# The opening of a conformer block's first FFN: x by token tile, the first adaLN pair on TensorE, paired first weight tiles, and a longer ramp of row tiles

## The chip, the cores and the metric

The kernel runs on one core of one Trainium2 chip. Its time is device microseconds per execution, the median of several runs. Beside the times stands one profiled execution, whose trace gives every instruction's start, duration and what it waited for. The engines are named as in the profile: PE (TensorE matmul), PEld (TensorE weight load), DVE (VectorE), ACT (ScalarE), POOL (GpSimd) and SP, whose queue issues all the loads here.

## What is computed

One conformer block on 256 tokens of width 2048, in float32. A conditioning vector `c` gives nine modulation vectors (adaLN): shift, scale and gate for each of the three parts.

```python
c_act = silu(c)                                     # [1, 2048]
ada = c_act @ w_ada + b_ada                         # nine vectors of 2048
h = modulate(rms_norm(x, ffn1_norm), sh1, sc1)      # h * (1 + sc1) + sh1
x = x + 0.5 * g1 * swiglu(h, w_gu, w_down)          # FFN 1: 2048 -> 2 x 5632 -> 2048
h = modulate(rms_norm(x, mix_norm), shm, scm)
x = x + gm * hybrid_mixer(h, ...)                   # differential attention and causal convolution
h = modulate(rms_norm(x, ffn2_norm), sh2, sc2)
x = x + 0.5 * g2 * swiglu(h, ...)                   # FFN 2
```

The first product of FFN 1 needs the normalised x (a sum over all 2048 channels of a token), transposed to channels on partitions, and for its first 128 channels 128 values of the scale `sc1` and 128 of the shift `sh1`. Each of these values is a sum over all 2048 entries of `silu(c)`.

## The kernel before

**Products.** A float32 product with weights is three passes of a rounded type: each operand is split into a high part and its exact remainder, and hi\*hi, hi\*lo and lo\*hi are accumulated (`mm3`, lines 232 to 234). A weight tile is four row tiles of 128 x 512, 1 MB, loaded into one of four buffers `raw` (line 217); per two row tiles ACT casts the high part (line 222) and DVE subtracts it to get the low part (line 224). With two token tiles a row tile costs PE 2 x 3 products.

**adaLN tiles.** An adaLN tile is 128 outputs by 2048 inputs, 1 MB; there are 144, in the order in which they are needed: for each 128-channel tile a scale and a shift. `ada(j)` loads a tile into a `raw` buffer (line 151), multiplies it on DVE with `silu(c)`, which lies on every partition (`c_bc`), and sums along the row (line 152). Every second tile DVE adds the biases (line 156); `modulation` makes the scale column from it (line 184). `ada_until(j)` issues all tiles up to j, `ada_share(r, limit)` adds r to a credit and issues a tile for each whole one.

**The opening.** `c` is loaded as one row, spread to all partitions by products with a row of ones (line 110) and passed through silu on ACT (line 112). Then x is loaded by column quarters for both token tiles (line 569), with sums of squares on ACT and DVE (lines 252, 255), then the constants, among them the biases and the identity for transposes. `Norm.begin` makes the reciprocal root (lines 268, 128, 129), scales x (line 280) and transposes it on PE (line 285); `Norm.tile` modulates one 128-channel tile of one token tile on DVE (line 293), casts it on ACT (line 295) and takes the remainder on DVE (line 296).

**FFN.** The first projection is cut into 22 chunks of 512 columns (256 gate, 256 up), each with a 2048-row weight matrix, that is four pieces of four row tiles. Stage A takes the first row tiles of every chunk and evacuates the sum into `parts` (line 345): 1, 1, 1, 2, 2, 2, 3 (five times), then 4 row tiles (`EXT`), since the modulations of the first piece's four row tiles arrive one after the other. Loads go three chunks ahead of the products (`AHEAD`). Then `n_a2` = 8 chunks, from the fourth on, get the rest of their first piece and their second piece (the last `n_a3` = 2 of them the third too) and DVE adds this to `parts` (line 412); then all chunks are finished. `pieces()` makes the activations of the second and third piece (lines 282, 285, 314, 317 to 319) as soon as their adaLN tiles are issued.

**Order.** The tile framework's planner orders each engine's instructions, by program order and by its own estimate of when operands are ready; each engine then works in that order. `tc.issue_after(ins)` puts instructions of a block behind `ins` on its engine. A tile name's buffers are reused in turn, and a load into one waits until its last reader is done. `blk` buffers (32 of 4 KB per partition) hold x, parts, activations and more.

Of the kernel before, what the change touches and what calls it, by code (L numbers as in the profile page):

```python
# [16 lines left out]
F32 = mybir.dt.float32  # L17
# [30 lines left out]
# columns of the packed small parameters  # L48
# [17 lines left out]
def block_kernel(ctx: ExitStack, tc: tile.TileContext, x_in, c_in, pos_in, w_ada, small, w_gu1, w_dn1,  # L66
# [3 lines left out]
    blkp = ctx.enter_context(tc.tile_pool(name="blkp", bufs=32))  # L70
# [30 lines left out]
    # ---------------------------------------------------------------- constants  # L101
    c_bc = const.tile([P, D], F32, name="c_bc")
    c_row = [blk([1, 1024]) for _ in range(2)]
    ones_r = tmp([1, P])
    nc.gpsimd.memset(ones_r, 1.0)
    for i in range(2):
        nc.sync.dma_start(out=c_row[i], in_=c_in[:, i * 1024:(i + 1) * 1024])
        for j in range(2):
            pc = acc_tile()
            nc.tensor.matmul(pc, ones_r, c_row[i][:, j * 512:(j + 1) * 512], start=True, stop=True)  # L110
            o = (2 * i + j) * 512
            nc.scalar.activation(out=c_bc[:, o:o + 512], in_=pc, func=AF.Silu)
    cst = const.tile([P, NCOLS], F32, name="cst")
    pos_i = const.tile([P, NT], I32, name="pos_i")

# [8 lines left out]
    nc.gpsimd.memset(half, -0.5)  # L124

    def rstd_of(ss, n, count, eps):
# [16 lines left out]
    # ---------------------------------------------------------------- adaLN projections  # L143
    ada_cols = {}

    def ada(j):
        g = j // 8
        if j % 8 == 0:
            ada_cols[g] = const.tile([P, 8], F32, name=f"ada{g}")
        raw = rawp.tile([P, D], F32, tag="raw", name=nm("raw"))  # L150
        nc.sync.dma_start(out=raw, in_=w_ada[j])
# [6 lines left out]
    ada_next = [0]  # L158
# [18 lines left out]
    def modulation(base, k, norm):  # L177
        """Scale and shift columns of the 128-channel tile k."""
# [9 lines left out]

    def gate(base, scale):
        """The gate's 2048 values on every partition, as four [P, 512] views (through DRAM)."""  # L190
# [755 lines left out]
```

## Time and profile before

| | |
|---|---|
| time, median of 3 runs | 1874.07 us (1871.6 to 1874.78) |
| profiled execution: span from the first to the last instruction | 1872.4 us |
| what the runs' median has beside that span | 1.7 us |
| mean granted TensorE clock | 0.995 |
| first product of FFN 1 | at 21.79 us |
| moved by DMA | 495.92 MB, 265 GB/s |

The profiled execution's own time is not listed beside its span; the three runs' times are what there is, and the span lies within them. In the rows, L224 is line 224 of the kernel, `wlo<-raw,whi` are the written and the read buffers by name, and `[2.41 <-ACT whi L222]` is idle time of the engine before the instruction and what ended it. In rows of stretches the busy times stand by engine, then the granted clock as a share of full speed, the DMA engines' share and GB/s.

### The profile page before, as it was taken

The numbers are of one execution on the slowest core, as the hardware profiler recorded it, in microseconds if no ns is written. First come the engines' busy times: TensorE is split into PE (matmuls) and PEld (weight loads), VectorE is DVE, ScalarE is ACT, GpSimd is POOL, SyncE is SP. The second block draws the span as 40 slices with busy tenths as digits, with TensorE's granted clock in tenths as the row PEclk, the third lists the DMA queues.
The fourth block names the chain that finished last, engine by engine and source line by source line (L and its number), as shares of the span: only waits on it lengthen the run. The fifth ranks groups of instructions, "written<-read, shape, count | busy, mean of one in ns | idle before, by whom it ended". The sixth has DMA issues, their size and how long they took to land.

```text
span 1872.4 us, 21954 instructions
## 1 busy us (share of the span) xinstructions
PE 1838.1 (98%) x8295; PEld 1510.8 (81%) x8295; DVE 1439.3 (77%) x1921; ACT 905.5 (48%) x1363; POOL 30.9 (2%) x34
## 2 busy tenths in 40 slices
PE   6999999999999999999999999999999999999999
PEld 3788888888888888778877788888888888888887
DVE  6779889988888777789999688775877755544443
ACT  4654354444444434454876555654444444433332
POOL 0000000000000000000110100000000000000000
PEclk9999999999999999999999899999999999999999
DMA  8888978888898888646343696895777755555552
GB/s 312 341 315 328 364 272 327 330 326 329 317 345 330 335 340 333 226 170 210 137 158 138 241 344 257 328 355 202 274 285 272 275 197 180 190 215 205 201 212 79
DMA packets 72141, 495.92 MB, mean 265 GB/s; under 512 B 8114, under 2 KB 8290, under 8 KB 14052
## 3 DMA queue, kind: packets, MB, share of 16 engines
q1 hardware_dynamic: 72036, 494.53, 71.5%
q8 instruction: 65, 1.06, 0.2%
q14 instruction: 40, 0.33, 0.1%
HBM read 492.37 MB, written 2.12 MB: 264 GB/s over the span
## 4 chain that ended last, share of the span: by engine, by line
PE 91%; DVE 5%; ACT 2%; issue 1%; DMA 1%; POOL 1%; POOLq 0%; ACTq 0%; DVEq 0%
PE acc L233 29%; PE acc L234 29%; PE acc L232 29%; DVE wlo L224 1%; DVE blk L596 1%; PE tp L426 1%; DMA raw<-in_w_ada_dram 1%; PE acc L677 1%; DVE raw L152 1%; PE tp L285 0%; ACT whi L222 0%; PE acc L110 0%; PE tp L740 0%; POOL rs L129 0%; ACT tmp L632 0%
## 5 line engine op out<-in xcount | busy, mean ns | idle before, releaser
L222 ACT CAST whi<-raw 128x1024 fp32r<-128x1024 f32 (+1 forms) x624 | 645.7, 1042 | 773.1 <-PE acc L234 665.9
L224 DVE TENSOR_TENSOR wlo<-raw,whi 128x1024 fp32r<-128x1024 f32 (+1 forms) x624 | 747.5, 1210 | 349.6 <-ACT whi L222 348.6
L232 PE MATMUL acc<-whi,blk 128*128 128x512 f32 x2464 | 966.2, 394 | 12.2 <-ACT whi L222 6.2
L233 PE MATMUL acc<-wlo,blk 128*128 128x512 f32 x2464 | 965.1, 392 | 3.5 <-DVE wlo L224 3.5
L234 PE MATMUL acc<-whi,blk 128*128 128x512 f32 x2464 | 964.8, 392 | 0.5 <-DVE blk L319 0.5
L232 PEld LDWEIGHTS acc<-whi,blk 128*128 128x128 f32 x2464 | 464.2, 189 | 110.0 <-ACT whi L222 8.3
L233 PEld LDWEIGHTS acc<-wlo,blk 128*128 128x128 f32 x2464 | 464.9, 189 | 101.6 <-DVE wlo L224 6.7
L234 PEld LDWEIGHTS acc<-whi,blk 128*128 128x128 f32 x2464 | 464.8, 189 | 97.3 <-DVE blk L319 0.9
L152 DVE CUSTOM_DVE_ANT_0 raw<-raw,c_bc 128x2048 f32<-128x2048 f32 x144 | 328.9, 2285 | 5.2 <-DMA raw<-in_w_ada_dram 5.2
L596 DVE SCALAR_TENSOR_TENSOR blk<-blk,cst,blk 128x256 f32<-128x256 f32 x240 | 100.9, 483 | 0.0
L345 ACT COPY blk<-acc 128x512 f32<-128x512 f32 x88 | 51.0, 589 | 84.6 <-PE acc L234 81.3
L422 DVE TENSOR_TENSOR blk<-acc,blk 128x512 f32<-128x512 f32 x88 | 56.8, 684 | 0.5 <-PE acc L234 0.5
L233 PE MATMUL acc<-blk,blk 128*128 128x512 f32 x96 | 37.4, 391 | 0.5 <-DVE blk L224 0.5
L232 PE MATMUL acc<-blk,blk 128*128 128x512 f32 x96 | 37.8, 394 | 0.0
L234 PE MATMUL acc<-blk,blk 128*128 128x512 f32 x96 | 37.4, 390 | 0.0
L424 DVE TENSOR_TENSOR blk<-blk 128x256 f32<-128x256 f32 x88 | 34.7, 420 | 0.8 <-ACT blk L423 0.7
L423 ACT ACTIVATE blk<-blk 128x256 f32<-128x256 f32 x88 | 33.3, 409 | 2.6 <-DVE blk L422 1.7
L244 DVE TENSOR_TENSOR blk<-tp,blk 128x512 fp32r<-128x512 f32 x44 | 30.0, 685 | 0.9 <-ACT blk L243 0.8
L224 DVE TENSOR_TENSOR blk<-raw,blk 128x1024 fp32r<-128x1024 f32 x24 | 28.7, 1221 | 0.8 <-ACT blk L222 0.8
L426 PEld LDWEIGHTS tp<-cst,blk 128*128 128x128 f32 x176 | 21.6, 140 | 5.6 <-DVE blk L244 0.3
L243 ACT CAST blk<-tp 128x512 fp32r<-128x512 f32 x44 | 25.3, 581 | 1.6 <-PE tp L426 1.6
L426 PE MATMUL tp<-cst,blk 128*128 128x128 f32 x176 | 26.0, 272 | 0.0
(134 smaller groups left out, 624.1 us busy)
## 6 DMA issues: line engine op xcount, KB each, us to landing
raw<-in_w_gu_dram SPq DMA_DIRECT2D x165, 1024.0 KB, 4.9
raw<-in_w_ada_dram SPq DMA_DIRECT2D x144, 1024.0 KB, 5.7
raw<-in_w_dn_dram SPq DMA_DIRECT2D x88, 1024.0 KB, 4.8
raw<-in_w_in_dram SPq DMA_DIRECT2D x40, 1024.0 KB, 4.8
raw<-in_w_out_dram SPq DMA_DIRECT2D x16, 1024.0 KB, 5.4
raw<-in_w_gu_dram SPq DMA_DIRECT2D x8, 768.0 KB, 7.0
raw<-in_w_gu_dram SPq DMA_DIRECT2D x6, 512.0 KB, 6.6
blk<-gate_line SPq DMA_DIRECT2D x6, 512.0 KB, 6.6
```

The lines of the kernel that those rows point to most:

```text
L152: nc.vector.tensor_tensor_reduce(out=raw, in0=raw, in1=c_bc, scale=1.0, scalar=0.0, op0=ALU.mult, op1=ALU.add, accum_out=ada_cols[g][:, j ...
L222: nc.scalar.copy(out=hi[:, :m, :], in_=raw[:, h:h + m, :])
L224: nc.vector.tensor_sub(out=lo[:, :m, :], in0=raw[:, h:h + m, :], in1=hi[:, :m, :].bitcast(F32))
L232: nc.tensor.matmul(acc, ah, wh, start=start, stop=False)
L233: nc.tensor.matmul(acc, ah, wl, start=False, stop=False)
L234: nc.tensor.matmul(acc, al, wh, start=False, stop=stop)
L345: last_part[0] = nc.scalar.copy(out=parts[c][:, t, :], in_=accs[t])
L422: nc.vector.tensor_add(out=p[:, t, :], in0=accs[t], in1=p[:, t, :])
L423: nc.scalar.activation(out=p[:, t, :256], in_=p[:, t, :256], func=AF.Silu)
L424: nc.vector.tensor_mul(out=p[:, t, 256:], in0=p[:, t, :256], in1=p[:, t, 256:])
L426: nc.tensor.transpose(tp[:, i, t * P:(t + 1) * P], p[:, t, 256 + i * P:256 + (i + 1) * P], ident)
L596: nc.vector.scalar_tensor_tensor(out=y, in0=u, scalar=w, in1=y, op0=ALU.mult, op1=ALU.add)
```

## The change

- `c` is loaded as 128 x 16 columns; silu runs on these. `c_bc` is made by 16 transposes on PE (a column broadcast along the free axis) and four ACT copies.
- The order of loads is `c`, constants, x by token tile in halves of 1024 columns (512 KB each), then the first adaLN pair. x lies in an own buffer; `blk` has 28 buffers for its 32.
- `first_modulation`: the weights of the first scale and shift tile are stored by input row, `w_ada0`, [128, 16, 256], and loaded in quarters and eighths into `blk` buffers. PE sums them, 16 row tiles for each of the two, with a column of silu(c) as the moving operand. DVE makes scale and shift from the two PSUM columns. The load of the first weight pair stands ahead of the last two eighths.
- `Norm.tile` takes both token tiles at once, and the high part comes from the transposed x in PSUM on ACT directly, beside DVE's.
- `w_pair` loads the first row tile of two chunks at once (512 KB) into a `blk` buffer, and ACT and DVE split both together.
- `EXT` is eight chunks with 1 row tile, four with 2, three with 3. The adaLN tiles of the opening are put by a table (`FIRST_ADA`: after which load how many), then by the share of 0.78 per load.
- `n_a2` is 12 and `n_a3` 4 in FFN 1. adaLN tile numbers begin at 2, since `w_ada` no longer holds the first two.

```diff
+PAIRS = 4
-EXT = (1,) * 3 + (2,) * 3 + (3,) * 5
+EXT = (1,) * (2 * PAIRS) + (2,) * 4 + (3,) * 3
+FIRST_ADA = {1: 1, 2: 1, 4: 1, 5: 1, 7: 1, 8: 1, 9: 1, 10: 1}
...
+    nc.sync.dma_start(out=c_col, in_=c_in)
+    nc.sync.dma_start(out=cst[:, :first_cols], in_=small[:, :first_cols])
+    for t in range(NT):
+        for h in range(2):
+            nc.sync.dma_start(out=xall[:, t, 1024 * h:1024 * h + 1024],
+                              in_=x_in[t * P:(t + 1) * P, 1024 * h:1024 * h + 1024])
...
+            nc.tensor.transpose(pc[:, j * P:(j + 1) * P], c_col[:, k:k + 1].to_broadcast([P, P]), ident)
+        nc.scalar.copy(out=c_bc[:, i * 512:(i + 1) * 512], in_=pc)
...
+    def first_modulation(between):
...
+        ps = [acc_tile((P, 1)) for _ in range(2)]
+        for k0, n in ((0, 4), (4, 4), (8, 4), (12, 2), (14, 2)):
+            if k0 == 12:
+                between()
+            wa = blk([P, 4, 2 * P])
+            nc.sync.dma_start(out=wa[:, :n, :], in_=w_ada0[:, k0:k0 + n, :])
+            for k in range(n):
+                for i in range(2):
+                    nc.tensor.matmul(ps[i], wa[:, k, i * P:(i + 1) * P], c_col[:, k0 + k:k0 + k + 1],
+                                     start=k0 + k == 0, stop=k0 + k == KT - 1)
+        G, SH = scales[:, 0:1], ada_cols[0][:, 1:2]
+        nc.vector.scalar_tensor_tensor(out=G, in0=ps[0], scalar=bias1, in1=col("n1")[:, 0:1], op0=ALU.add, op1=ALU.mult)
+        nc.vector.tensor_add(out=SH, in0=ps[1], in1=cst[:, p0 + 1:p0 + 2])
...
+    def w_pair(c):
+        raw = blk([P, 2, 512])
+        w_dma[0] = nc.sync.dma_start(out=raw, in_=w_gu1[c:c + 2, 0].rearrange("c p n -> p c n")[:, :, :512])
...
+        nc.scalar.copy(out=hi, in_=raw)
+        nc.vector.tensor_sub(out=lo, in0=raw, in1=hi.bitcast(F32))
...
+            hi = self.hh[k // 4][:, k % 4, ts]
+            nc.scalar.activation(out=hi, in_=src, func=AF.Identity, scale=G, bias=SH)
+            nc.vector.tensor_scalar(out=hf, in0=src, scalar1=G, scalar2=SH, op0=ALU.mult, op1=ALU.add)
+            self.last = nc.vector.tensor_sub(out=self.hl[k // 4][:, k % 4, ts], in0=hf, in1=hi.bitcast(F32))
...
+            first_modulation(lambda: load(0))
+            begin_ready()
+            for i in range(len(loads) + AHEAD):
+                if i < len(loads):
+                    if i:
+                        load(i)
                     with tc.issue_after(w_dma[0].ins):
-                        ada_share(ada_a[0] * ext[c] / 4, ada_a[1])
+                        if i < 11:
+                            ada_until(ada_next[0] + FIRST_ADA.get(i, 0))
+                        else:
+                            ada_share(ada_a[0], ada_a[1])
+                        begin_ready()
...
-    ffn(norm1, w_gu1, w_dn1, 32, (0.78, 32), (0.74, 100), norm_m, 8, 2)
+    ffn(norm1, w_gu1, w_dn1, 32, (0.78, 32), (0.74, 100), norm_m, 12, 4)
```

More of the change, by code (lines that the diff above doesn't have):

```diff
@@ L99, in tp_tile @@
         return tpp.tile(list(shape), F32, tag="tp", name=nm("tp"))
[L102 to L112, printed above, removed]
+    c_col = const.tile([P, KT], F32, name="c_col")
     cst = const.tile([P, NCOLS], F32, name="cst")
     pos_i = const.tile([P, NT], I32, name="pos_i")
+    xall = const.tile([P, NT, D], F32, name="xall")
+    x = [xall[:, :, n * 512:(n + 1) * 512] for n in range(4)]
+    first_cols = _COLS["nm"][0]
+    nc.sync.dma_start(out=c_col, in_=c_in)
[4 more added lines that the diff above has]
+                              in_=x_in[t * P:(t + 1) * P, 1024 * h:1024 * h + 1024])
     def col(name):
@@ L124, in block_kernel @@
     nc.gpsimd.memset(half, -0.5)
+    nc.scalar.activation(out=c_col, in_=c_col, func=AF.Silu)
+    c_bc = const.tile([P, D], F32, name="c_bc")
+    for i in range(4):
+        pc = acc_tile()
+        for j in range(4):
+            k = 4 * i + j
+            nc.tensor.transpose(pc[:, j * P:(j + 1) * P], c_col[:, k:k + 1].to_broadcast([P, P]), ident)
+        nc.scalar.copy(out=c_bc[:, i * 512:(i + 1) * 512], in_=pc)
     def rstd_of(ss, n, count, eps):
@@ L227, in w_tile @@
         return lambda j: views[j]
+    def w_pair(c):
+        raw = blk([P, 2, 512])
+        w_dma[0] = nc.sync.dma_start(out=raw, in_=w_gu1[c:c + 2, 0].rearrange("c p n -> p c n")[:, :, :512])
+        hi = whp.tile([P, 2, 512], F32R, tag="whi", name=nm("whi"))
+        lo = wlp.tile([P, 2, 512], F32R, tag="wlo", name=nm("wlo"))
+        nc.scalar.copy(out=hi, in_=raw)
+        nc.vector.tensor_sub(out=lo, in0=raw, in1=hi.bitcast(F32))
+        return [lambda j, i=i: (hi[:, i, :], lo[:, i, :]) for i in range(2)]
     def mm3(acc, a, w, start, stop):
@@ L244, in split_from_psum @@
         nc.vector.tensor_sub(out=lo, in0=tp, in1=hi.bitcast(F32))
-    x = []
     def square_sum(n, t, dst, vec=False):
@@ L353, in pieces @@
                             st.piece(kb, t)
-        begun = 4 * bool(st.done)
         ext = [4] * NCH
         if not st.done:
-            sts = [st.begin(0, t, True) for t in range(NT)]
-            ws = []
-            for c in range(NCH + AHEAD):
-                if c < NCH:
-                    ext[c] = EXT[c] if c < len(EXT) else 4
-                    while begun < ext[c]:
-                        with tc.issue_after(w_dma[0].ins) if c else nullcontext():
-                            ada_until(base + 2 * begun + 2)
-                        for t in range(NT):
-                            st.done.add((0, t))
-                            st.tile(sts[t], 0, t, begun)
-                        begun += 1
-                    ws.append(w_tile(w_gu[c, 0], False, (0, ext[c])))
-                    with tc.issue_after(w_dma[0].ins):
-                        ada_share(ada_a[0] * ext[c] / 4, ada_a[1])
-                if c >= AHEAD:
-                    cc = c - AHEAD
-                    stage_a(cc, ws[cc], [acc_tile() for _ in range(NT)], (0, 1), ext[cc])
+            raws, begun = st.begin_both(), [0]
@@ new lines, in ffn, with load, begin_ready @@
+            loads = [(2 * i, 2 * i + 1) for i in range(PAIRS)] + [(c,) for c in range(2 * PAIRS, NCH)]
+            ws = {}
+            def load(i):
+                cs = loads[i]
+                if len(cs) == 2:
+                    ws[cs[0]], ws[cs[1]] = w_pair(cs[0])
+                else:
+                    ws[cs[0]] = w_tile(w_gu[cs[0], 0], False, (0, ext[cs[0]]))
+            for c in range(NCH):
+                ext[c] = EXT[c] if c < len(EXT) else 4
+            def begin_ready():
+                while begun[0] < 4 and base + 2 * begun[0] + 2 <= ada_next[0]:
+                    st.tile(raws[begun[0]], tmp([P, S]), (begun[0], slice(0, S)))
+                    begun[0] += 1
@@ L566, in block_kernel @@
     norm2 = Norm(96, "n2", sm([P, NT, 4], "ss"))
[L567 to L577 removed]
+    for t in range(NT):
+        for n in range(4):
+            square_sum(n, t, norm1.ss, n % 2 == 1)
+    ffn(norm1, w_gu1, w_dn1, 32, (0.78, 32), (0.74, 100), norm_m, 12, 4)
     st = norm_m
```

61 lines of the change are left out of this document (34 added, 27 removed).

## The prediction

> **What bounds the kernel now.** I read the page first, then busy time by stretch of the opening, then the chain of waits and the timeline of the same microseconds.
>
> ```profile
> span 1872.4 us, 21954 instructions
> PE 1838.1 (98%) x8295; PEld 1510.8 (81%) x8295; DVE 1439.3 (77%) x1921; ACT 905.5 (48%) x1363; POOL 30.9 (2%) x34
> ```
>
> TensorE (PE) is busy for all but 34.3 us of the span. A change that leaves the products as they are can win only among those, or lose by making new ones. Where they lie (columns: stretch, length, then busy time of PE, PEld, DVE, ACT, POOL with instruction counts, granted clock, DMA share, GB/s):
>
> ```profile
> 0.00:9.70 9.70, 7.16 (x8) 2.49 (x8) 1.49 (x5) 3.26 (x5) 0.43 (x6) 1.00 0.70 231
> 9.70:14.90 5.20, 0.69 (x3) 0.69 (x4) 3.03 (x12) 2.85 (x9) 1.11 (x2) 1.00 1.03 428
> 14.90:21.79 6.89, 1.28 (x7) 0.88 (x6) 6.84 (x12) 2.81 (x6) 0.00 (x0) 1.00 0.51 155
> 21.79:52.23 30.44, 23.11 (x75) 16.43 (x75) 21.30 (x31) 15.64 (x27) 0.00 (x0) 0.89 0.93 350
> 52.23:64.00 11.77, 11.77 (x52) 9.74 (x53) 11.54 (x17) 7.16 (x13) 0.00 (x0) 1.00 0.85 329
> ```
>
> From 52.23 on PE has no idle time, at 11.77 / 52 = 0.226 us a product. Before 52.23 it has done 74 products (three chunks of 6, three of 12, one of 18, two of the next; the 75th begins at the border), worth 74 x 0.226 = 16.7 us. So the opening **loses 52.2 - 16.7 = 35.5 us**. That is the purse. How it is spent, by the chain of waits and the timeline:
>
> ```profile
> 2.31 7.17 PE acc L110 x8
> 10.53 2.04 ACT tmp L255 x7
> 14.71 1.67 DVE raw L152
> 16.92 2.20 DVE raw L152
> 19.76 6.63 DMA raw<-in_w_ada_dram
> 31.04 7.72 DMA raw<-in_w_ada_dram
> 45.60 0.43 PE acc L232
> ```
>
> ```profile
> 5.22 12.05 SPq L217 DMA_DIRECT2D raw<-in_w_gu_dram  x3
> 14.21 1.97 PE L285 MATMUL tp<-cst,tmp 128*128 128x128 f32 x8 [4.73 <-DVE tmp L280]
> 16.35 1.26 ACT L222 CAST whi<-raw 128x512 fp32r<-128x512 f32 x2 [3.80 <-DMA raw<-in_w_gu_dram]
> 19.05 0.69 DVE L224 TENSOR_TENSOR wlo<-raw,whi 128x512 fp32r<-128x512 f32 x1
> 21.79 0.79 PE L232 MATMUL acc<-whi,blk 128*128 128x512 f32 x1 [5.61 <-ACT blk L295]
> 23.23 0.63 PE L232 MATMUL acc<-whi,blk 128*128 128x512 f32 x1
> 25.30 0.40 PE L234 MATMUL acc<-whi,blk 128*128 128x512 f32 x1
> 29.35 0.73 PE L232 MATMUL acc<-whi,blk 128*128 128x512 f32 x2 [1.62 <-ACT whi L222]
> 41.80 0.84 PE L232 MATMUL acc<-whi,blk 128*128 128x512 f32 x2 [2.41 <-ACT whi L222]
> 43.53 0.79 PE L233 MATMUL acc<-wlo,blk 128*128 128x512 f32 x1 [0.89 <-DVE wlo L224]
> 52.23 0.50 PE L233 MATMUL acc<-wlo,blk 128*128 128x512 f32 x1 [0.52 <-DVE wlo L224]
> ```
>
> Two adaLN reductions on DVE hold the first product until 21.79. The third weight load is issued only when the first reduction frees a buffer, so the DMA queue stands nearly still (155 GB/s from 14.9 to 21.8), and later chunks wait for adaLN tiles that came late (6.63 and 7.72 us). PE pays twice: after its waits the products are slow (0.63 us each and 0.43 apart, as at 23.23 and 45.60, against 0.40 and 0.226).
>
> **The change, part by part.**
>
> *Loads.* The buffers of the first pair no longer come from the four `raw` ones, so the queue doesn't stop. Bytes up to the first quarter of the pair's matrix: c 8 KB, constants 147, x 2097, quarter 524, together 2777 KB. By 9.70 us 231 x 9.7 = 2241 KB are in, the rest at 428 GB/s is there at 10.95. The lag to first use I take from the first weight tile: bytes ahead of it 4612 KB, in at about 15.35 by the same rates, its cast starts at 16.35: 1.0 us. So the quarters can be used at about 11.95, 13.2 and 14.4, and after the first weight pair the two eighths at 16.2 and 16.9 us. The 8 products of L110 and the broadcast of c leave; 16 transposes take their place, at 1.97 / 8 = 0.25 us 4.0 us on a PE that has nothing else until 11.95: nothing, and if that cover is gone, 4 us.
>
> *The pair on PE.* 16 row tiles times 2, float32 with one moving column. Nothing runs so in the opening, but the convolution's channel mean does:
>
> ```profile
> L740 PE MATMUL tp<-tmp,blk 128*128 128x1 f32 x64 | 7.7, 250 | 0.0
> 1038.93 2.07 PE L740 MATMUL tp<-tmp,blk 128*128 128x1 f32 x18
> 1052.10:1052.40 0.30, 0.30 (x5) 0.30 (x5) 1.00 0.84 355
> 1052.70:1053.00 0.30, 0.30 (x3) 0.30 (x2) 0.50 0.00 0
> ```
>
> Its 32 products are 64 instructions (two each), 18 of them in 2.07 us, about 0.107 apart. So the pair is 64 instructions as well: **6.9 us** at full clock. But within such a stream the granted clock falls to 0.50 (last row), and then 5 instructions in 0.3 us become 2 or 3. I take twice the price, 0.213 each, **13.65 us**, because PE is slow at the start (first products 0.43 apart) and these rows show that such a stream doesn't hold the clock up. Then PE, not DMA, is last: 11.95 + 13.65 + 0.85 for the last four transposes of x among them (half of 8 in 1.97, rounded down) = **26.45**, where the data would be done at 17.8.
>
> The Trainium skill ("TensorE: Matmul & The Clock Gate", section "LDWEIGHTS (loading the stationary operand)") gives a weight load of 128 columns 128 / 1.2 = 107 ns, with no word of the clock's state; by it the pair would be done at 17.8, the second rival below. The row at granted clock 0.50 speaks against it.
>
> Durations for what follows (DVE, then ACT, groups of the first 180 us):
>
> ```profile
> L224 DVE TENSOR_TENSOR wlo<-raw,whi 128x1024 fp32r<-128x1024 f32 x48 | 57.4, 1221 | 20.4 <-ACT whi L222 20.1
> L152 DVE CUSTOM_DVE_ANT_0 raw<-raw,c_bc 128x2048 f32<-128x2048 f32 x24 | 54.7, 2287 | 3.9 <-DMA raw<-in_w_ada_dram 3.9
> L224 DVE TENSOR_TENSOR wlo<-raw,whi 128x512 fp32r<-128x512 f32 x12 | 8.2, 688 | 0.0
> L412 DVE TENSOR_TENSOR blk<-acc,blk 128x512 f32<-128x512 f32 x12 | 8.0, 687 | 1.6 <-PE acc L234 1.6
> L293 DVE TENSOR_SCALAR tmp<-tp,scales,ada 128x128 f32<-128x128 f32 x8 | 2.9, 407 | 0.1
> L296 DVE TENSOR_TENSOR blk<-tmp,blk 128x128 fp32r<-128x128 f32 x8 | 2.1, 288 | 0.1
> L184 DVE SCALAR_TENSOR_TENSOR scales<-ada,cst 128x1 f32<-128x1 f32 x12 | 1.9, 158 | 0.3
> L222 ACT CAST whi<-raw 128x1024 fp32r<-128x1024 f32 x49 | 50.2, 1053 | 18.5 <-DMA raw<-in_w_gu_dram 12.3 <-PE acc L234 4.5 <-DVE wlo L224 1.7
> L317 ACT ACTIVATE tmp<-tp,ada,scales 128x128 f32<-128x128 f32 x8 | 3.4, 454 | 5.6 <-DVE scales L184 5.6
> L318 ACT CAST blk<-tmp 128x512 fp32r<-128x512 f32 x4 | 2.4, 616 | 0.0
> L282 ACT ACTIVATE tmp<-blk,rstd 128x512 f32<-128x512 f32 x4 | 2.9, 725 | 0.0
> ```
>
> *First product.* After 26.45: scale and shift 2 x 0.16, the new ACT pass over 256 columns (between 454 for 128 and 725 for 512: 0.55), hand-overs: 1.2 us, so it starts at about **27.7**, six later than now.
>
> *What is queued behind that wait.* DVE and ACT work in order. Scale and shift stand ahead of the second weight pair's split and of adaLN tiles 2 and 3, whose data land between 18 and 26 us by the same count of bytes, so DVE stands idle and starts in arrears. Its work from 26.45 until the first full chunk (number 15) can run: first tile 1.75 with hand-overs; wait for the next cast 0.5; seven splits 8.55; three of 1.22 + 0.69, 5.7; half of chunk 15's, 1.2; eight reductions at 2.29 and a hand-over, 19.0; four bias adds and scales, 1.9; three tiles at about 0.5 + 0.4, 2.7. Sum **41.3**, to 67.7. PE alone has 8 x 6 + 4 x 12 + 3 x 18 = 150 products until there: 33.9 us, and 8 x 0.2 = 1.6 for the slow first ones, from 27.7: 63.2. DVE is later. Two or three products of chunk 15 go ahead of its low part (0.4). Loss then: 67.7 - 0.4 - 33.9 = **33.4 us**. The buffers don't bind harder: the ninth chunk's load waits for adaLN tile 2 (32.3) and is needed at 42.
>
> *After stage A.* By the shares adaLN stands at 15 tiles when stage A ends; the second group of activations needs 16. So it comes at the head of the next stage, its ACT work queued behind the last evacuation: two normalisations 0.72, two scalings 0.45 and a cast 0.62 per token tile, beside two weight casts at 1.05, 7 us in all, while PE has 18 + 8 instructions, some 4.9 us. With the first products going ahead: **1.7 us** new (0.5 to 3). Four more chunks get a second pass: 8 adds of 0.687 on DVE, under PE's products; uncovered 5.5 us. The rest is as before; two reductions fewer on DVE and some five adaLN tiles moved to later stages are under products too.
>
> *Sum.* 33.4 + 1.7 = 35.1 against 35.5: **-0.4 us**. The runs' median, 1874.07, lies 1.7 above the profiled span; I add the difference to the median: about **1873.5**.
>
> **The rivals.**
>
> *DVE goes on during the wait.* If the planner puts the second split and the reductions of tiles 2 and 3 ahead of scale and shift, 9.5 us of arrears go and PE sets the pace: loss 27.7 + 1.6 + 1.7 = 31.0, so -4.5 us, **1869.5**. For it: a weight tile's split did overtake bias and scale now (19.05). Against: those data were there; here the load of tile 2 is issued after the last eighth.
>
> *The pair is done when its data are* (17.8). DMA sets the pace then: 15.5 MB from there to chunk 15 at 350 / 0.93 = 376 GB/s from 15.9 on is 41.1, lag 1.0, cast and split of half a tile 2.3: 60.3; loss 60.3 - 33.9 - 0.4 + 1.7 = 27.7, **1866.3**. Against: the row at clock 0.50.
>
> *Slower: the clock falls again.* In my forecast PE waits 4 us for DVE between 38 and 68, in pieces up to 1.7. Now a wait of 2.41 us, two products and 0.89 more cost the clock (43.53 to 49: 14 products at 0.2 more, 2.8 us). From one wait of about 3 us on, that is 1.5 + 2.8 more: **1878**. For it: DVE and ACT are in arrears together. Against: a wait of 1.62 us (29.35) kept the clock.
>
> *Nothing gained because the transfer is hidden anyway* gives the forecast's time and isn't told apart by it.
>
> **How the numbers follow.** What a measurement can tell from no change is 0.2%, 3.7 us: 1870.3 to 1877.8. Forecast 0.54, own range 1870 to 1877 (pair's end 1 us, DVE's chain 1.5, new wait 0.5 to 3), of it faster 0.08, slower 0.03; DVE goes on 0.17, three quarters faster; data set the end 0.14, all faster; clock falls 0.15, slower in 0.12, the rest same. Faster 0.36, same 0.47, slower 0.17 with roundings. Range **1865.5 to 1878.0**, from below the second rival to the slower one.
>
> **What would show it.** The pair: 64 instructions, 0.2 us apart, ending near 26.5 (0.107 and 18: second rival). First product at 27 to 28. DVE: a wait of several us on PE ahead of the scale, then no idle time until about 65; reductions ahead of it: first rival. A granted clock of 0.50 between 30 and 70: third. Waits of 1 to 3 us some 18 products after the last evacuation of stage A. Wrong altogether if PE's loss ahead of 70 us is under 30 or over 38 us.

## The result, and the profile after

The changed kernel takes **1891.24 us** (median of 4 runs, 1889.68 to 1894.5) against 1874.42 us (1871.6 to 1875.46) of the kernel before on the same chip: ratio 1.0092, 95% interval 1.0078 to 1.0106. It is slower by about 17 us; 1873.5 was forecast, with 1878 as the upper end.

The page after, first two lines:

```profile
span 1888.3 us, 22081 instructions
PE 1849.2 (98%) x8367; PEld 1523.7 (81%) x8367; DVE 1439.4 (76%) x1917; ACT 908.0 (48%) x1359; POOL 30.8 (2%) x33
```

PE is 98% busy in both kernels, so this share says nothing here; and it is busy for 11 us more, 10 of them in the opening: the pair (13.66 us) and the 16 transposes for `c_bc` (3.65) came in, the products with the row of ones (7.16) left. The stretches of the opening (columns as in the prediction) say more:

```profile
20.00:28.00 8.00, 8.00 (x38) 7.93 (x38) 0.22 (x1) 0.00 (x0) 0.00 (x0) 1.00 1.03 409
28.00:40.00 12.00, 11.15 (x42) 9.04 (x42) 10.75 (x15) 9.95 (x16) 0.00 (x0) 1.00 0.45 154
40.00:60.00 20.00, 16.75 (x69) 12.30 (x68) 15.72 (x17) 12.28 (x21) 0.00 (x0) 1.00 0.85 303
60.00:80.00 20.00, 15.93 (x67) 11.90 (x67) 16.09 (x21) 10.96 (x16) 0.00 (x0) 1.00 0.96 344
80.00:110.00 30.00, 30.00 (x134) 24.86 (x133) 23.63 (x25) 16.27 (x22) 0.00 (x0) 1.00 0.94 360
28.00:75.10 47.10, 38.94 (x153) 29.19 (x153) 37.66 (x48) 31.22 (x50) 0.00 (x0) 1.00 0.78 275
```

Until 28 us PE sums the pair, and DVE and ACT stand still but for 0.22 us. (The clock column has 1.00 here, though the pair's instructions come 0.213 us apart, twice the 0.107 of the mixer's; that PE is slow in the opening is read from this spacing, not from the column.) From 28.87 on PE makes products, with gaps until 75.1 us (before: 52.2). By then it has started 152 (the count of the last row less the pair's end), worth 152 x 0.226 = 34.4 us: the opening **loses 75.1 - 34.4 = 40.7 us**, where 33.4 were forecast and the kernel before lost 35.5. The timeline of PE, then DVE, then ACT in these microseconds, with what each waited for:

```profile
12.71 1.12 PE L346 MATMUL tp<-cst,tmp 128*128 128x128 f32 x4 [4.76 <-DVE tmp L344]
13.62 3.42 PE L212 MATMUL acc<-c_col,blk 128*128 128x1 f32 x16
17.78 10.24 PE L212 MATMUL acc<-c_col,blk 128*128 128x1 f32 x48
28.87 0.80 PE L272 MATMUL acc<-whi,blk 128*128 128x512 f32 x1 [0.85 <-ACT blk L332]
48.89 0.73 PE L272 MATMUL acc<-whi,blk 128*128 128x512 f32 x2 [0.94 <-ACT whi L252]
50.15 0.50 PE L273 MATMUL acc<-wlo,blk 128*128 128x512 f32 x1 [0.53 <-DVE wlo L254]
27.63 0.22 DVE L215 SCALAR_TENSOR_TENSOR scales<-acc,bias,cst 128x1 f32<-128x1 f32 x1 [8.60 <-PE acc L212]
48.87 1.23 DVE L254 TENSOR_TENSOR wlo<-raw,whi 128x1024 fp32r<-128x1024 f32 x1 [0.94 <-ACT whi L252]
73.82 4.63 DVE L254 TENSOR_TENSOR wlo<-raw,whi 128x1024 fp32r<-128x1024 f32 x4 [2.51 <-ACT whi L252]
47.30 0.59 ACT L394 COPY blk<-acc 128x512 f32<-128x512 f32 x1 [2.07 <-PE acc L274]
47.79 1.05 ACT L252 CAST whi<-raw 128x1024 fp32r<-128x1024 f32 x1
71.58 1.26 ACT L394 COPY blk<-acc 128x512 f32<-128x512 f32 x2 [2.81 <-PE acc L274]
72.74 4.07 ACT L252 CAST whi<-raw 128x1024 fp32r<-128x1024 f32 x4
```

What is to be seen is a ring. At 47.30 ACT evacuates a chunk, after 2.07 us of waiting for PE to finish it. Behind it in ACT's queue stands the cast of the next weights, which starts at once at 47.79: its load had landed at 43.86, and it had waited for nothing but its turn. At 48.87 DVE, idle for 0.94 us, gets that cast and makes the low part; PE, idle at 48.89 for the cast and at 50.15 for the low part, goes on. The same happens at the casts at 55.27 and 61.86, whose loads had landed at 52.06 and 58.26. So the loads lie ready, each engine has work, and yet all wait for one another in turn: PE's end, evacuation, cast, low part, PE. The last and largest turn, 71.58 to 75.10, is another case: the load for the cast at 72.74 had landed only at 72.25. It was issued at 64.79, when a buffer came free, and took 7.5 us, so that an earlier turn on ACT could have brought that cast 0.5 us. The chain of waits goes round the ring (start, length, what; the 0.46 us called issue are the evacuation that ACT starts at 54.78):

```profile
54.52 0.24 PE acc L274
54.81 0.46 issue
55.27 1.06 ACT whi L252
56.35 1.23 DVE wlo L254
57.63 0.50 PE acc L273
```

The Trainium skill ("TensorE: Matmul & The Clock Gate", section "Architectural detail: the array is 16× 32×32, not 1× 128×128") says that ACT's and DVE's queues are strictly first in, first out. This trace agrees: the cast at 47.79, whose data lay there from 43.86 on, didn't pass the evacuation that waited 2.07 us.

After stage A the forecast wait is there (1.30 + 0.97 us, and 0.28 for a cast between them), and a like one ahead of the third group of activations, not forecast:

```profile
114.32 1.27 PE L323 MATMUL tp<-cst,tmp 128*128 128x128 f32 x8 [1.30 <-ACT tmp L320]
117.57 0.50 PE L273 MATMUL acc<-wlo,blk 128*128 128x512 f32 x1 [0.97 <-DVE wlo L254]
193.09 0.66 PE L323 MATMUL tp<-cst,tmp 128*128 128x128 f32 x4 [1.54 <-ACT tmp L320]
```

**How the 16 us of span divide.** The first transpose of the first gate, which ends stage two of FFN 1, is a mark that every variant has (one line's instructions: count, shortest/mean/longest ns, first start to last end). Before, then after:

```profile
L197 PE MATMUL tp<-cst,gate x3: 271/271/421, 545.2 to 1644.5; 128*16 128x128 f32 x3
```

```profile
L227 PE MATMUL tp<-cst,gate x3: 271/271/417, 554.8 to 1660.5; 128*16 128x128 f32 x3
```

**9.6 us** are lost ahead of the mark, and 1888.3 - 554.8 = 1333.5 against 1872.4 - 545.2 = 1327.2, that is **6.3 us**, behind it, in stages whose code the change hardly touches. In the 9.6 the opening has 40.7 - 35.5 = 5.2, and the waits of 2.55 + 1.54 us after stage A, less 0.4 that the kernel before had there, 3.7; the 0.7 that is left is less than one execution scatters.

### The profile page after: what moved, and what is told of

Same layout as the page of the kernel before. It is cut to its first block, busy times and chain, and to the rows that moved or that the text cites. A ratio compares the mean times of both kernels' runs of the same rounds, so it can differ in the third digit from the quotient of the medians.

```text
span 1888.3 us, 22081 instructions
## 1 busy us (share of the span) xinstructions
PE 1849.2 (98%) x8367; PEld 1523.7 (81%) x8367; DVE 1439.4 (76%) x1917; ACT 908.0 (48%) x1359; POOL 30.8 (2%) x33
## 4 chain that ended last, share of the span: by engine, by line
PE 88%; DVE 6%; ACT 2%; DMA 2%; issue 2%; POOL 1%; SPq 0%; POOLq 0%; ACTq 0%; DVEq 0%
PE acc L273 28%; PE acc L274 28%; PE acc L272 28%; DVE wlo L254 2%; DVE blk L656 1%; PE tp L491 1%; PE acc L212 1%; ACT whi L252 1%; PE acc L737 1%; DVE raw L161 0%; DMA xall<-in_x_dram 0%; PE tp L800 0%; DMA raw<-in_w_ada_dram 0%; PE tp L323 0%; DMA raw<-in_w_in_dram 0%
## 5 line engine op out<-in xcount | busy, mean ns | idle before, releaser
L252 ACT CAST whi<-raw 128x1024 fp32r<-128x1024 f32 x619 | 642.7, 1045 | 767.6 <-PE acc L274 661.6
L254 DVE TENSOR_TENSOR wlo<-raw,whi 128x1024 fp32r<-128x1024 f32 x619 | 740.5, 1209 | 341.2 <-ACT whi L252 340.1
L161 DVE CUSTOM_DVE_ANT_0 raw<-raw,c_bc 128x2048 f32<-128x2048 f32 x142 | 324.2, 2285 | 8.7 <-DMA raw<-in_w_ada_dram 8.6
L293 ACT ACTIVATE tmp<-xall 128x512 f32<-128x512 f32 x20 | 12.7, 633 | 30.0 <-DVE xall L528 15.3
```

Source lines behind the costliest of these rows:

```text
L161: nc.vector.tensor_tensor_reduce(out=raw, in0=raw, in1=c_bc, scale=1.0, scalar=0.0, op0=ALU.mult, op1=ALU.add, accum_out=ada_cols[g][:, j ...
L252: nc.scalar.copy(out=hi[:, :m, :], in_=raw[:, h:h + m, :])
L254: nc.vector.tensor_sub(out=lo[:, :m, :], in0=raw[:, h:h + m, :], in1=hi[:, :m, :].bitcast(F32))
```

## The experiments

All times are medians; "mark" is the start of the first gate's transposes and "rest" the span from there to the end, of the profiled execution. One execution scatters: the kernel before and a variant of it that is the same program up to the mark have it at 545.2 and 543.0. So differences under 2 us in one profile are not read.

**1. The pair back on DVE.** One row of weights per output, in halves of 1024, summed on DVE with `c_bc`.

```diff
-        ps = [acc_tile((P, 1)) for _ in range(2)]
...
+        for q in range(4):
+            i, h = q % 2, q // 2
+            if q == 3:
+                between()
+            wa = blk([P, 1024])
+            nc.sync.dma_start(out=wa, in_=w_first[i, :, 1024 * h:1024 * h + 1024])
+            nc.vector.tensor_tensor_reduce(out=wa, in0=wa, in1=c_bc[:, 1024 * h:1024 * h + 1024], ...)
```

> The changed kernel with one part undone: the first scale and shift tile are summed on DVE again, as four halves of 128 x 1024 in buffers of their own (the loads stay where they are, so the DMA queue doesn't stop). Theory 1 (the slow pair on PE makes everything after it late, one to one): first product at 19 to 21 us instead of 28.87, and 7 to 9 us less than the changed kernel's 1891.2, so 1882 to 1884. Theory 2 (waits of DVE for casts that stand behind evacuations on ACT, 7.9 us in all, whenever the start is): the same five waits stay between the start and chunk 15, only earlier. Rival (full buffers and DMA set the pace of the first chunks): the start comes earlier but chunk 15 doesn't, gain under 3 us.

1881.4 us (ratio to before 1.0038, 1.0023 to 1.0052): 9.8 less than the change and 0.6 below theory 1's range. The first product is at 21.16 instead of 28.87, the mark at 547.8 instead of 554.8, the rest 1333.3. So **the pair on TensorE costs 7 us at the mark**, though not a microsecond of it shows as idle PE. The ring's waits are all still there, 6.3 us earlier, as theory 2 has it:

```profile
21.16 0.79 PE L273 MATMUL acc<-whi,blk 128*128 128x512 f32 x1 [6.17 <-ACT blk L333]
67.57 0.73 PE L273 MATMUL acc<-whi,blk 128*128 128x512 f32 x2 [1.62 <-ACT whi L253]
68.83 0.50 PE L274 MATMUL acc<-wlo,blk 128*128 128x512 f32 x1 [0.53 <-DVE wlo L255]
```

**2. The cast ahead of the evacuation.** In stage A a chunk's evacuation goes behind the first cast of the next load on ACT.

```diff
-                last_part[0] = nc.scalar.copy(out=parts[c][:, t, :], in_=accs[t])
+                with tc.issue_after(after.ins) if after else nullcontext():
+                    last_part[0] = nc.scalar.copy(out=parts[c][:, t, :], in_=accs[t])
...
+                                casts[i - AHEAD + 1] if i - AHEAD + 1 < len(loads) else None)
```

> The changed kernel, with the evacuation of each chunk in stage A put behind the first cast of the next load on ACT. Theory 2: PE's waits of 1.5 to 2.2 us ahead of five chunks between 45 and 75 us go, the start of chunk 15 comes 5 to 7 us earlier (73.8 now), time 1884 to 1886. Theory 1 and the rival (buffers, DMA): the casts wait for their data instead, at the same times; within 1.5 us of 1891.2.

1885.07 us (1.0056, 1.0041 to 1.0071), 6.2 less than the change. PE's waits from the first product to 80 us, after and here (waited for; total, times, longest):

```profile
PE acc L272 <- ACT whi L252: 4.9, 4, 1.6
PE acc L273 <- DVE wlo L254: 2.4, 5, 0.5
```

```profile
PE acc L277 <- DVE wlo L258: 2.5, 6, 0.8
PE acc L276 <- ACT whi L254: 1.3, 1, 1.3
ACT whi L254 <- DMA raw<-in_w_gu_dram: 8.3, 4, 4.0
```

PE's waits for casts go from 4.9 to 1.3 us, and stage A ends at 108.2 instead of 112.4 (1.0 of it because this execution began earlier). The first product of the first full chunk, 73.84 after, comes at 69.90: 3.9 earlier, where 5 to 7 were expected. The last line, of ACT's waits in the same stretch, has the reason: the casts now wait for their loads, 8.3 us in all, where in the changed kernel none of them waited 0.1 us. So the order was what held them, and right behind it stand the loads; the wait of 1.3 us that is left is for a cast at 59.04 whose load landed at 58.97. By the mark, at 552.7, only 2.1 are left. Behind stage A PE waits about as in the changed kernel (1.29, 0.28 and 0.83 us for 1.30, 0.28 and 0.97), but in this execution the clock fell, and the products from 113.98 to 118.68 came 0.43 us apart:

```profile
110.00:120.00 10.00, 8.76 (x28) 6.38 (x29) 8.80 (x11) 8.30 (x15) 0.00 (x0) 0.66 0.46 143
```

**3. Both.**

> The changed kernel with both edits that were tried alone: the first adaLN pair summed on DVE again, and in stage A each chunk's evacuation put on ACT behind the first cast of the next load. My theory: the two losses are separate (the chain of DVE starts late because PE sums the pair at 0.213 us an instruction; and on its way DVE waits for casts that stand behind evacuations), so the gains of 9.8 and 6.2 us add: about 1875, 1873.5 to 1877, with stage A ending near 102 instead of 112.4 and no idle time of DVE over 0.5 us ahead of a cast. Rival: once DVE starts sooner, what comes next is the arrival of the weights, and the order of the casts is worth little: 1879 to 1881.

1880.3 us (1.003, 1.0019 to 1.0041), not the sum but in the range of the rival, the arrival of the weights: until 80 us ACT's casts of row tiles wait 6.6 us for loads, up to 2.4. At the mark the order is still worth 3.9 us: it is at 543.9, 10.9 ahead of the change. Up to there both gains are had, and **the opening is no longer slower than before** (545.2). But the rest stays at 1333.2. The whole was 11 us better than the change and still slower than the kernel before; what was left lay behind the mark.

**4. The order of work in a 128-wide tile put back** (DVE scales, then ACT rounds), for the hand-over to the mixer, where PE is busy for 65.8 of the 70 us from 760 on (and of those from 771 on) instead of 67.6.

```diff
-                    self.tile(tp[:, j, :], hf[:, j, :], (4 * kb + j, slice(t * P, (t + 1) * P)))
+                    nc.vector.tensor_scalar(out=hf[:, j, :], in0=tp[:, j, :], scalar1=G, scalar2=SH, ...)
+                    nc.scalar.copy(out=hi, in_=hf[:, j, :])
```

> The changed kernel with the former order of one modulated tile (DVE first, then the cast on ACT from its result) where a layer's first activations are made at the end of the layer before; the opening keeps the new one. If the new tile makes the 2.1 us that are lost between the end of FFN 1 and the first convolution chunk, that step is gone (first convolution transposes 9.6 us later than in the kernel before instead of 11.7) and the time is 2 to 4 us less, 1887 to 1889; the opening is as it is. Rival (the planner's order there comes from other parts): no change at the junction.

1889.53 us (1.0084, 1.0065 to 1.0102), and PE is busy for 65.67 of those 70 us: not the cause.

**5. adaLN tile 16 in stage A.** `credit[0] = 0.6` ahead of the opening.

> The changed kernel with a credit of 0.6 at the start of the shares, so that the sixteenth adaLN tile is issued in stage A. If the missing tile makes the wait at the end of stage A (2.5 us at 113 us), it goes and the time is 2 to 3 us less, 1888 to 1889. Rival (the tile's reduction on DVE takes as much elsewhere): the wait moves and the time stays.

1889.3 us (1.0083, 1.0068 to 1.0098). The waits behind stage A go from 4.1 to 1.9 us and the hand-over comes back (67.73 of 70), but the opening pays: the granted clock is 0.89 from 60 to 90 us, where it was 1.00.

**6. More adaLN tiles per weight tile**, 0.81 for 0.74, in the rest of FFN 1.

> The changed kernel with one number changed: from the second stage of the first FFN on, 0.81 adaLN tiles go with a weight tile instead of 0.74, so that its 100 tiles are done some seven weight tiles sooner. My theory for the loss at the hand-over to the mixer: three reductions (one before) and the planner's place for them fall into the first row tiles of the mixer. Then PE is busy for 67.5 us of the 70 from 760 on again instead of 65.8, and the time is 1888 to 1889.5. If the 4 us at the mixer's end come from the same shift, 1884 to 1886. Rival: the hand-over's loss has nothing to do with adaLN tiles: 1890.5 to 1892.5.

1897.57 us (1.0118, 1.0103 to 1.0134), slower by 6: all of my readings missed. Of the down projection's 50 us from 650 on PE is busy for 48.33, and ACT waits for the weights:

```profile
650.00:700.00 50.00, 48.33 (x211) 39.07 (x210) 38.43 (x41) 19.03 (x22) 0.00 (x0) 1.00 0.85 332
```

```profile
ACT whi L252 <- DMA raw<-in_w_dn_dram: 41.6, 13, 5.3
```

(The changed kernel has 3 such waits there, 7.3 us in all, up to 2.6, and PE is busy throughout.)

My reason for it (three reductions fall into the 70 us after 760 instead of one) was an error of reading as well: the window was fixed, the changed kernel 11 us later. Counted from the mixer's own first transposes, the last reduction ahead of them starts about equally early in both (9.0 us before, 10.6 after).

**7. The longer opening alone, in the kernel before.**

```diff
-EXT = (1,) * 3 + (2,) * 3 + (3,) * 5
+EXT = (1,) * 8 + (2,) * 4 + (3,) * 3
...
-    ffn(norm1, w_gu1, w_dn1, 32, (0.78, 32), (0.74, 100), norm_m, 8, 2)
+    ffn(norm1, w_gu1, w_dn1, 32, (0.78, 32), (0.74, 100), norm_m, 12, 4)
```

> The kernel before with one part of the change alone: the chunks of stage A begin with 8x1, 4x2, 3x3 rows of tiles instead of 3x1, 3x2, 5x3, and 12 chunks (four of them with three pieces) get the second pass instead of 8 (two). Pair on DVE, loads of x and single weight row tiles as before. My theory: PE has 48 products instead of 18 before it needs the second adaLN pair, so most of the waits of 6.6 and 7.7 us for adaLN tiles go; the loss of the opening falls from 35.5 to 28 to 31 us; about 1.7 us come back as the wait for the second group of activations at the end of stage A, and some 2 us at the hand-over to the mixer if adaLN tiles are left over: 1869 to 1873, and the harm in the change is the pair on TensorE. Rival: the longer opening itself is the harm, since it puts 30 evacuations ahead of casts on ACT and reductions of adaLN tiles into later stages: 1878 or more.

1899.04 us (1.0129, 1.0112 to 1.0146), 24 us slower: the rival, and the largest loss of all. The mark is at 553.4 (+8.2), the rest 1342.4 (+15.2). I took it for the culprit, which the next run refuted.

**8. The shorter opening in the changed kernel.**

```diff
-PAIRS = 4
-EXT = (1,) * (2 * PAIRS) + (2,) * 4 + (3,) * 3
+PAIRS = 2
+EXT = (1,) * (2 * PAIRS) + (2,) * 3 + (3,) * 4
```

and 8, 2 for 12, 4 as above.

> The changed kernel with the longer opening alone undone as far as it can be: chunks begin with 4x1, 3x2, 4x3 rows instead of 8x1, 4x2, 3x3 (two weight pairs instead of four), and 8 chunks, two of them with three pieces, get the second pass, as in the kernel before. The pair on TensorE, x by token tile and the paired loads stay. Theory A, from the run of the kernel before with the longer opening alone (24 us slower): the longer opening is the harm, and the time falls to 1874 to 1880. Theory B, my prediction's: PE needs the products of the longer opening while DVE reduces adaLN tiles, so that without them it waits longer ahead of the second and third row tile: 1892 to 1898.

1892.41 us (1.01, 1.0085 to 1.0115); mark 554.3, rest 1334.5. Theory A is out; theory B's range begins where there is no difference. In the changed kernel the longer opening is worth nothing and costs nothing; what it costs the kernel before isn't a term that can be carried over, and why is not shown.

**9. The second pass alone, in the kernel before** (12, 4 for 8, 2, with the rows as they were).

> The kernel before with the other half of the longer opening alone: 12 chunks instead of 8 get a second pass, four of them (two) with three pieces; the rows with which chunks begin stay 3x1, 3x2, 5x3. It tells which half made the kernel before 24 us slower. If it is the second pass (eight more adds on DVE, more chunks at the adaLN tiles' due dates): 1882 to 1895. If it is the rows with which the chunks begin: 1873 to 1877.

1883.44 us (1.0053, 1.0037 to 1.007). So the second pass has about 10 of the 24 us; the other half, the rows, was not run alone. The mark is at 541.9, *ahead* of before, and the rest 1338.5: 11.3 us lost behind the mark by an edit ahead of it.

**10. The shorter opening with edits 1 and 2.**

> The changed kernel with three edits together: the shorter opening of the run beside it, the first adaLN pair summed on DVE, and each chunk's evacuation behind the first cast of the next load. What stays of the change is x by token tile, c as a column, the paired loads for four chunks and the new order of adaLN tiles. Theory A: the three parts are the whole harm, and their gains add (at least 11, 10 and 5 us on 1891): 1863 to 1870, faster than both kernels. Theory B: the shorter opening costs what the other two bring: 1878 to 1884.

1876.89 us (1.0018, 1.0008 to 1.0027). Its mark, 541.2, is among the earliest here; its rest is 1335.4. Not the sum of theory A, since the shorter opening had nothing to give, and better than theory B.

**11. Edits 1, 2 and 5 together.**

> The changed kernel with the pair on DVE, the evacuations behind the casts, and the adaLN shares set so that tile 16 falls into stage A. It has the longer opening. Alone, the last edit took away 2.2 us of waits at the end of stage A and 2 us at the hand-over to the mixer and gave as much back in the opening. Theory: with DVE earlier it gives less back: 1875.5 to 1878.5, still not faster than the kernel before. Rival: 1879 to 1882, the same as without it.

1879.36 us (1.0033, 1.0022 to 1.0043), the rival. Its ten runs spread from 1874.63 to 1884.58, and its profile (span 1872.8) is of the quickest, 4.7 us below the median: its rest, 1330.7, is not typical.

**12. Edit 2 in the kernel before.**

> The kernel before with only ACT's order in stage A changed: each chunk's evacuation stands behind the first cast of the next chunk's load. My theory: the order is a loss of the change far more than of the kernel before, where PE's waits for casts in the opening are 5.8 us in four places and two of these come from late loads, not from the queue: 1872 to 1873.5, not more than 2.5 us gained. Rival: it is a loss of both alike, then 1868 to 1870.

1871.08 us (0.9984, 0.9975 to 0.9994), faster than both kernels, by a little more than I expected. Every instruction of PE, and DVE's and ACT's last 1100 and 650, stand behind the mark in the same order as before; the rest is 1329.3.

### The rest of the span, and the order of instructions

Edits of the opening and of stage two changed the rest, which lies behind them, by up to 15 us. The programs' order of PE's instructions behind the mark differs, too. Between the traces of before and after, 256 of 5983 stand elsewhere, in 36 places, all between 747 and 1291 us of the kernel before, that is from the last 20 us of the down projection through the mixer to the start of FFN 2. Kernels with one order, by PE, DVE and ACT alike, make up classes:

| order | kernels (experiments by number) | mark, us | rest, us |
|---|---|---|---|
| A | before; 12 | 545.2; 541.7 | 1327.2; 1329.3 |
| B | after; 1; 2; 3 | 554.8; 547.8; 552.7; 543.9 | 1333.5; 1333.3; 1329.9; 1333.2 |
| C | 4 | 555.0 | 1331.3 |
| D | 5; 11 | 556.5; 542.1 | 1330.6; 1330.7 |
| E | 8; 10 | 554.3; 541.2 | 1334.5; 1335.4 |
| own | 6; 7; 9 | 557.9; 553.4; 541.9 | 1340.1; 1342.4; 1338.5 |

Within a class the rest is mostly the same to about 2 us, whatever the opening did, but class B spans 3.6, and B, C and D overlap. So the table tells class A (1329.3 at most) from E and the kernels with orders of their own (1334.5 and more); B, the changed kernel's, it tells from A only in part. One place can be read in the timeline, the hand-over from FFN 1's down projection to the mixer. PE of the kernel before, then of the changed one, around the end of the first token tile's sum:

```profile
763.16 0.39 PE L233 MATMUL acc<-wlo,blk 128*128 128x512 f32 x1
...
767.69 0.39 PE L232 MATMUL acc<-blk,blk 128*128 128x512 f32 x1
767.92 0.60 PE L285 MATMUL tp<-cst,tmp 128*128 128x128 f32 x4
```

```profile
775.24 0.39 PE L272 MATMUL acc<-blk,blk 128*128 128x512 f32 x1
...
777.73 0.39 PE L274 MATMUL acc<-blk,blk 128*128 128x512 f32 x1
779.31 0.63 PE L323 MATMUL tp<-cst,tmp 128*128 128x128 f32 x4 [1.19 <-DVE tmp L318]
```

While DVE takes that sum, adds it to x and normalises it (4.1 to 4.6 us), PE before had 21 products of the other token tile left, 4.8 us; after it had 12, 2.7 us, since the planner had put some of them ahead. So it waits 1.19 us. The change's source doesn't ask for this.

Is it the order, or the five adaLN tiles that were late? At the start of the down projection 67 tiles are out in the kernel before and 62 in the changed one.

**13. One number in the kernel before**: the fraction of an adaLN tile due at the start of the down projection.

```diff
         gbc = None
+        if nxt is norm_m:
+            credit[0] = 0.4
```

> The kernel before, with one number set anew at the start of the first down projection: the fraction of an adaLN tile that is due there is 0.40 instead of 0.64 (67 tiles are out in both). Everything up to the gate, at 545 us, is the kernel before to the instruction; after it, the order of PE's instructions that the planner writes differs. Theory: the time from the gate's transposes to the end goes by that order and not by the work; it was 1327.2 us before, and 1330 to 1342 in every kernel with another order: here 1330 to 1337 too, and so 1876 to 1884 in all. Rival: the time after the gate goes by the number of adaLN tiles that are late, which is the same here: 1326 to 1329, and 1873 to 1875.5.

1871.64 us (0.9988, 0.9979 to 0.9997), rest 1326.6. The order is another, and the time isn't worse but a little better, 2.7 us (0.6 to 3.9 by the interval): my direction was wrong. That a new order costs something as such has fallen.

**14. The tiles put back in the changed kernel**: 0.85 of a tile per weight tile in stage two, 67.64 due at the down projection.

> The changed kernel with adaLN tiles put back to the plan of the kernel before by the start of the first down projection: 0.85 of a tile with each weight tile of the stage ahead of it (0.74 in the changed kernel), and the fraction due set to 0.64, so that 67 tiles are out there, as before, instead of 62. Theory of the order: the opening stays, the gate's transposes at about 555 to 557, and the time from there may be anything from 1327 to 1335 as the order falls out. Theory of the late tiles: it is 1327 to 1329 again, and the whole 1885 to 1887.

1891.6 us (1.0103, 1.0087 to 1.012), as without it; mark 555.9. (The profiled execution, span 1897.1, was the slowest of four; the others, at 1890.58 to 1892.57, put the rest near 1334.) The late tiles alone are not the cause in the changed kernel: they are out again, and the rest didn't come back (though the order is a new one once more). Kernel 8, with 67 tiles out and a rest of 1334.5, says the same.

**15. The fraction 0.64 in kernel 10.**

> The kernel with the shorter opening, the pair on DVE and the evacuations behind casts, with the adaLN fraction due at the start of the first down projection 0.64 instead of 0.40. It had 67 tiles out there already. Theory of the order: another order after the gate, another time from there: not the 1335.4 us it had, by 1.5 us or more; 1870 to 1875 if the order is the better one. Rival: fraction and order are without effect: 1876 to 1878.

1873.92 us (0.9999, 0.999 to 1.0008), rest 1330.7 for 1335.4: 3 us from one number that changes the order alone (that of a few loads and reductions too). The two kernels ran on different chips, and their intervals, each against the kernel before on its chip, just touch.

**16. The same, with the old order of work in 128-wide tiles** (edit 4).

> The kernel with the shorter opening, the pair on DVE and the evacuations behind casts, and two things more: the order of work in a norm's 128-wide tiles as in the kernel before (DVE's scaling, then ACT's rounding), and the adaLN fraction due at the start of the first down projection set to 0.64, as it is in the kernel before, with 67 tiles out. PE's order after the gate is then nearer to that of the kernel before than in any other variant here. Theory: the gate's transposes at 541 as measured without the two, and 1327 to 1331 from there: 1869 to 1873. Rival: the time after the gate stays at 1335: 1877.

1872.94 us (0.9993, 0.9984 to 1.0002), mark 541.6, rest 1330.1: inside what was expected, and not to be told from the kernel before.

**17. Edits 12 and 13 together, in the kernel before.**

> The kernel before with the two small edits that each made it a little faster: each chunk's evacuation in stage A behind the first cast of the next load (3.6 us less, all of it ahead of the gate), and the adaLN fraction due at the start of the first down projection 0.40 instead of 0.64 (2.7 us less). Theory: they lie in different stages, so they add: 1866.5 to 1869.5, faster than both kernels. Rival: the second gain was one of the order's accidents and does not stay when the opening shifts by 3.5 us: 1870 to 1873.

**1870.57 us** (0.9978, 0.9969 to 0.9987). It has the lowest median here, 3.9 us ahead of the kernel before and 20.7 ahead of the changed one, but isn't to be told from 12 (1871.08) and 13 (1871.64): the two gains do not add, and the rival was right. Its rest, 1327.7, agrees with 13's; its mark, 543.3, isn't ahead of 13's 543.0, though the profiled execution was the longest of eleven.

## Why the prediction was wrong, point by point

- **The pair on PE: right.** 64 instructions, 3.42 + 10.24 = 13.66 us (13.65 forecast), 0.213 apart at half speed; the end at 28.02 instead of 26.45, because the first quarter of its matrix landed at 12.81 and not at 10.95, behind which PE still had four transposes of x to finish: the pair starts at 13.62 instead of 11.95. By the Trainium skill's formula for a weight load ("TensorE: Matmul & The Clock Gate", section "LDWEIGHTS (loading the stationary operand)") the pair would have been done, by an estimate from its 107 ns, at 13.62 + 64 x 0.107 = 20.5. The trace contradicts it, with 0.213 us. (The 17.8 of the second rival is too early even at full clock: 6.9 us of instructions and 0.85 of transposes from 11.95 on end at 19.7.)
- **First product: right** to 1.2 us (27.7, measured 28.87). **DVE's wait ahead of the scale: right** (8.60 us, and no reduction ahead of it), so the first rival is out; the second is out by the pair's end. The third, a clock that falls again, is out in the changed kernel (1.00 from 28 to 80 us, and 0.23 us between products once the slow first ones are over at 32.9), though it took back part of the gains of experiments 2 and 5.
- **What failed first: "starts in arrears", then 41.3 us of work without a pause.** The work was sized well: DVE is busy for 37.66 of the 47.10 us from 28.00 to 75.10. But it is idle for 9.4 of them, where I had allowed 0.5, and 7.9 lie in five waits for ACT. I added up DVE's work and PE's work and took the larger; ACT, busy for 31.22 of 47.10, looked free. It is free in sum and late in order: its casts stand behind evacuations, most of which wait for PE. From 26.45 + 41.3 = 67.7: 1.6 for the late end of the pair, 3.1 less work, 8.9 more waiting: 75.1. Experiment 2 shows this cause for about 3 of the 8.9 us (the first full chunk 3.9 earlier, 1.0 of it from the earlier start), taking PE's 4.9 us of cast waits down to 1.3. The rest stays: the largest wait, 2.51 us of DVE, was for a cast whose load had landed 0.5 us ahead of it, and with the casts put first ACT waits 8.3 us for loads. The sum has no term for late loads. Only the second rival counts them, and has those up to the first full chunk in at 57; that chunk's landed at 72.25, since it had waited for a buffer until 64.79 and found the DMA engines 96% busy.
- **What failed with it: the price of a late first product.** I weighed six later against the buffers that no longer stop the queue and found 2 us gained. Experiment 1 shows that they are paid at the mark, 7.0 us for a first product 7.7 us earlier: the loss of the late start was real, and the gain that was to stand against it was not, as the loads came early and then stood in full buffers (154 GB/s from 28 to 40 us, in the row above).
- **The wait after stage A: right** in place and kind, 2.55 us for 1.7 (0.5 to 3); its sister at 193.09 (1.54 us) was missed.
- **What failed second: "the rest is as before".** The span behind the mark has 6.3 us more, with the same products. That the five adaLN tiles stay under products fits experiment 14; what I left out is that the planner writes one order for the whole program, and that edits at its start reorder the mixer, 500 us later. Experiments 13 and 15 have such a reordering alone move the time, by some 3 us, at the edge of what the intervals tell; on top of edit 12 the same number brought 0.5 (experiment 17). Experiment 9 has a rest 11.3 us longer after an edit whose mark is earlier, but there 63 adaLN tiles are out instead of 67, too. That the order makes up the whole 6.3 us is not shown: one execution scatters by 2 us and in two kernels by more, and class B itself spans 3.6. The cause of this part stays open.
- **Left open:** why one order is better than another, beyond the place at the hand-over; why the longer opening costs the kernel before 8 us at the mark and the changed one nothing; what the rows alone cost; and what x by token tile and the paired loads are worth alone, which no run took out.
- **The range** was too narrow, and the prediction's own sign of being wrong altogether came, over 38 us lost: 40.7. It ended at 1878, from waits of 3 us that would cost the clock. Neither failed step was among its cases: each rival was one event in the opening, none a ring of waits, and none lay behind it.

## What to carry to other kernels

Adding up each engine's work and taking the largest is a lower bound; ahead of it, follow one tile through the queues of all engines that it passes, and ask at each what stands in front of it and what that waits for. An engine that is half idle can still set the pace, if the work that others need stands behind work that waits for them; moving the urgent instruction ahead of the patient one is then a small edit, and the only one here that made the tuned kernel faster by itself in the opening. It also uncovers what stands next in line, here the loads, so that the gain is smaller than the waits it removes. Where a planner orders the program, split every measurement at a mark behind the change: a gain in the changed stage and a loss in an untouched one look like one number otherwise.

## What was not expected of the hardware

- The granted clock fell without any single long wait: in the changed kernel with tile 16 in stage A it is 0.89 from 60 to 90 us; in the one with casts ahead 0.66 from 110 to 120. The Trainium skill ("TensorE: Matmul & The Clock Gate", section "HAM oscillation — how this bites in real kernels") names idle gaps of more than some 3.4 us; these runs show the fall with several shorter ones close together. Nor does their sum alone decide: waits of 1.40 and 0.53 us in a row at 63 us were followed by the fall with tile 16 in stage A and left the clock at 1.00 in the changed kernel, and so with 1.29, 0.28 and 0.83 us (casts ahead, fallen) against 1.30, 0.28 and 0.97 (changed kernel, 1.00). The four executions of the changed kernel alone have mean clocks from 0.988 to 0.996. What decides is not shown.
- 0.07 adaLN tiles more per weight tile, some 73 KB in the 5.4 us of its 24 products, went with waits of PE in the down projection (experiment 6), though the DMA engines are 85 to 89% busy there, no more than in the changed kernel (87 to 90%): between 600 and 750 us ACT waits for 13 loads, up to 5.3 us, instead of 3, up to 2.6. That the mean share leaves a tenth free did not mean that the next load came in time. Whether the loads or the new order of the instructions made the waits, this run doesn't tell.
